# Reordering the input projections of a two-layer hybrid trunk, and storing the normalised gating values in DRAM

## The chip, the cores and the metric

The kernel runs on one core of a Trainium2 chip. The metric is the device time of one execution in microseconds; the median of a few runs stands for a kernel, and lower is better. One execution was also recorded by the hardware profiler, and all rows below come from that one.

## The reference

Two layers are applied to 1024 prompt tokens and 8 x 16 sample tokens (1152 columns), with D_MODEL 1024. Each layer is `x + w_out @ (concat(A, B, C, D) * silu(gates))`, and all inputs of the four branches and the gates come from one projection of `rms_norm(x)`.

- A is RWKV-7 time mixing. A token shift mixes each column with the one before; a decay `exp(-exp(w_log))` and a rate `a` come from two low-rank projections; the normalised keys kk enter as `-kk` and `kk*a`; the recurrence is

```python
sa = einsum('bhij,bhj->bhi', s, -kk_t)
s = s * w_t[:, :, None, :] + sa[:, :, :, None] * (kk_t * a_t)[:, :, None, :] + v_t[:, :, :, None] * k_t[:, :, None, :]
y = einsum('bhij,bhj->bhi', s, r_t)
```

- B is latent attention with a block-causal mask. The change does not touch it.
- C is spatial gating. The values are layer-normalised over their 256 features (`vn`, of which the sample part is an output), mixed within chunks of 128 positions by a lower-triangular 128x128 matrix per head, and multiplied into u.
- D is pooling: trailing means over 2, 4, 8 or 16 tokens minus the token, a small linear map per group and a scale.

## The kernel before

Features lie on partitions and tokens on columns, in three groups g of 384 columns. A layer has 24 input projections of 128 features each. WDAD holds the decay's and the rate's low-rank inputs, K0 K1, R0 R1 and V0 V1 are keys, receptances and values of A, D0 D1 the inputs of D, GD0 GD1 its gates, VC0 VC1 the gating values of C, U0 U1 its u, GC0 GC1 its gates. `F_ORDER` is the order in which `project` runs them and in which their weights are loaded. Arithmetic is float32: weights and inputs are split in a high and a low part, and each product is three matmuls (high by high, low by high, high by low), so a projection is 3 groups x 8 x 3 = 72 matmuls of 128x384. The weights come by SP's DMA queue in quarters of 128 KB (tile wr, three buffers), ACT copies the high part (wh, L241), POOL subtracts for the low part (wl, L242).

All other work is written as generators in three lanes, "a", "v" and "n". `project` calls `tick()` at the ticks that `inproj` gives it, and a tick runs each lane one step further, so a lane's instructions stand between the matmuls of the projection that runs at that time. Each engine then works its instructions off in order.

- Lane "a" first holds `a_elem`, the keys' chain, six per layer (two halves i, three groups g). It makes from w, a and k the four factors of the recurrence's matrices: `ar` (with -kk times the decay before the token, and later r times the decay), and `kb`. cs is the running sum of the decays within a chunk of 64, ex is exp(-cs), ei exp(+cs).
- `systems(g)` makes for each chunk of 64 tokens the matrix product that has to be inverted (tile ns, two buffers), masks it on DVE (L514) and stores it to DRAM (nd) by ACT's queue.
- `solve` loads them again, all side by side on partitions, inverts them on DVE by forward substitution (62 operations for 32 columns, L538 and L540; a smaller one for the samples first), copies the result transposed (L550) and stores both to DRAM (dd, L552 and L553) on ACT's queue.
- `recurrence` runs the 18 chunks, the two of the samples first. `prepare` loads a chunk's inverse (tt<-dd, L571, on SP), makes the masked products gm (L580) and the transposes kbt and vu (L590, L595), `advance` carries the state. `groupnorm` runs on lane "n" after chunks 5, 11 and 15.
- `normalise(j)` of lane "v" (L846 to L857) transposes a tile of 128 tokens of the gating values into a psum buffer (pool st, two buffers), takes mean and variance on DVE (L850, L852), scales (L855), and lets POOL apply the layer norm's weight and bias (L856, L857). The nine results stay in three m tiles; the m pool has eight buffers.

Psum has three pools: pj (2 buffers, the projections), st (2), b (4). `pool_in` computes D's windows on POOL and DVE, `silu` the gates on ACT (L756 to L758) and DVE.

Of the kernel before, what the change touches and what calls it, by code (L numbers as in the profile page):

```python
# [10 lines left out]
F32 = mybir.dt.float32  # L11
# [9 lines left out]
NS, SL = 8, 16  # L21
# [10 lines left out]
(WDAD, K0, R0, V0, K1, R1, V1, D0, GD0, D1, GD1, VC0, VC1, U0, GC0, U1, GC1,  # L32
 GB0, GB1, Q0, Q1K, CK, GA0, GA1) = range(NF)

F_ORDER = (WDAD, K0, K1, R0, R1, V0, V1, D0, GD0, D1, GD1, VC0, VC1, U0, GC0, U1, GC1,
           Q0, Q1K, CK, GB0, GB1, GA0, GA1)


# [10 lines left out]
def tile_trunk(ctx: ExitStack, tc: tile.TileContext, *aps):  # L49
# [37 lines left out]
    def nm(p):  # L87
        cnt[0] += 1
        return f"{p}_{cnt[0]}"
# [17 lines left out]
    def m_tile(cols=T):  # L107
        return mp.tile([128, cols], F32, tag="m", name=nm("m"))
# [16 lines left out]
    def go(lane, gen):  # L125
        lanes.setdefault(lane, deque()).append(gen)

    def start(lane, gen):
        next(gen)
        go(lane, gen)  # L130
# [15 lines left out]
    def finish(*names):  # L146
        while any([step(n) for n in names]):
            pass
# [8 lines left out]
    def gcols(g):  # L157
        return slice(g * G, (g + 1) * G)
# [186 lines left out]
    for l in range(L):  # L345
# [11 lines left out]
        def vcol(i):  # L357
            return vc[:, i:i + 1]
# [46 lines left out]
        def shifted(f, dest, after=None):  # L405
            inproj(f, shift_sink(f, dest, after))
# [17 lines left out]
        def chv(t):  # L424
            return t.rearrange("p (c s) -> p c s", s=64)

        def a_elem(i, g, k):
# [32 lines left out]
            if n < G:  # L460
                Po.tensor_copy(out=PendS[:, i, :].rearrange("p (c s) -> p c s", c=2),
                               in_=ex[:, nch:].rearrange("p c (s t) -> p c s t", t=SL)[:, :, :, SL - 1])
            V.tensor_tensor(out=rw, in0=cs, in1=rw, op=ALU.subtract)
            ep = rw
            A.activation(out=ep, in_=rw, func=AF.Exp, scale=-DECAY_C)
            ei = cs
            A.activation(out=ei, in_=cs, func=AF.Exp, scale=DECAY_C)
            yield

            kk = q  # L470
            V.scalar_tensor_tensor(out=kk, in0=k, scalar=vcol(V_KK + i), in1=q, op0=ALU.mult, op1=ALU.mult)
            V.scalar_tensor_tensor(out=ar[:, :, 0, :], in0=chv(kk), scalar=-1.0, in1=chv(ep),
                                   op0=ALU.mult, op1=ALU.mult)

            recip1p(av)
            yield
# [2 lines left out]
            for hh in range(2):  # L479
                pr = slice(64 * hh, 64 * hh + 64)  # L480
                V.tensor_tensor(out=kb[pr, :, hh, :], in0=chv(kk)[pr], in1=chv(t)[pr], op=ALU.mult)  # L481
            V.tensor_scalar(out=av, in0=av, scalar1=vcol(V_KA + i), scalar2=nv[:, 11 + i:12 + i],
                            op0=ALU.mult, op1=ALU.add)
            V.tensor_tensor(out=av, in0=av, in1=ei, op=ALU.mult)
            for hh in range(2):
                pr = slice(64 * hh, 64 * hh + 64)
# [336 lines left out]
            inproj(fg, sink_gd)  # L823


        def gating():
            sg = m_tile(1024)
            sgb = sg[:, 0:512].rearrange("p (a i t) -> p a i t", a=2, i=2)
            SY.dma_start(out=sgb, in_=sgub[l])
            sgg = sg[:, 512:1024].rearrange("p (a t) -> p a t", a=2)  # L830
            SY.dma_start(out=sgg, in_=sgugb[l])
            vraw = []
            for fv in (VC0, VC1):
# [3 lines left out]
                    A.activation(out=vr[:, gcols(g)], in_=ps, func=AF.Copy)  # L837
                inproj(fv, sink_v)
                vraw.append(vr)
            vn = [m_tile(1024), m_tile(1024), m_tile(1024)]  # L840

            def vnt(j):
                return vn[j // 4][:, (j % 4) * 256:(j % 4 + 1) * 256]

            def normalise(j):
                ps = st()[:, 0:256]  # L846
                for i in range(2):
                    PE.transpose(ps[:, i * 128:(i + 1) * 128], vraw[i][:, j * 128:(j + 1) * 128], ident)
                bs = smp.tile([128, 6], F32, tag="bs", name=nm("bs"))
                V.bn_stats(out=bs, in_=ps)  # L850
                mv = smp.tile([128, 2], F32, tag="mv", name=nm("mv"))
                V.bn_aggr(out=mv, in_=bs)  # L852
                rs = smp.tile([128, 1], F32, tag="rs1", name=nm("rs1"))
                rsqrt(rs, mv[:, 1:2], 1.0, ELN)
                V.tensor_scalar(out=vnt(j), in0=ps, scalar1=mv[:, 0:1], scalar2=rs, op0=ALU.subtract, op1=ALU.mult)  # L855
                Po.tensor_tensor(out=vnt(j), in0=vnt(j), in1=sgg[:, 0], op=ALU.mult)  # L856
                Po.tensor_tensor(out=vnt(j), in0=vnt(j), in1=sgg[:, 1], op=ALU.add)  # L857

            def norms():
                for j in range(9):  # L860
                    normalise(j)
                    if j % 2:
                        yield
                A.dma_start(out=vn_o[l], in_=vnt(8))
            go("v", norms())
            wst = m_tile(1024).rearrange("p (a h t) -> p a h t", a=2, h=4)
            SY.dma_start(out=wst[:, 0], in_=wsT[l])
            SY.dma_start(out=wst[:, 1], in_=wsS[l])
# [5 lines left out]
            for i, (fu, fg) in enumerate(((U0, GC0), (U1, GC1))):  # L874
# [2 lines left out]
                def sink_u(g, ps, u=u):  # L877
                    A.activation(out=u[:, gcols(g)], in_=ps, func=AF.Copy)
                inproj(fu, sink_u)
                finish("v")  # L880

                def sink_gc(g, ps, i=i, u=u):
                    t = silu(ps)
# [21 lines left out]
        def after_k1(g, zs):  # L905
            start("a", a_elem(1, g, zs))
            if g > 0:
# [2 lines left out]
        project([(l, WDAD), (l, K0)], xh, xl,  # L910
                [shift_sink(WDAD, lambda g: z6[:, gcols(g)], tanh_part),
                 shift_sink(K0, lambda g: zk0[:, gcols(g)], lambda g, zs: start("a", a_elem(0, g, zs)))])
        shifted(K1, lambda g: zk1[:, gcols(g)], after_k1)
        go("a", idle(4))
        go("a", systems(2))
        go("a", idle(4))
        go("a", solve())
        receptance(0, R0)
        receptance(1, R1)
        values(V0)  # L920
        values(V1)
        A.dma_start(out=shift_o[l], in_=sho)
        pool_in(0, D0)
        go("a", recurrence())
        pool_gate(0, GD0)
        pool_in(1, D1)
        pool_gate(1, GD1)
# [675 lines left out]
```

## Time and profile before

| | us |
|---|---|
| median of 3 runs | 1447.89 (1444.7 to 1640.55) |
| the profiled execution | 1447.32 |
| its span, first to last instruction | 1445.5 |
| PE busy | 1358.6 (94%) |
| DVE, ACT, POOL busy | 786.8, 746.6, 465.2 |
| mean granted clock of TensorE | 0.986 |

PE is the matrix engine (TensorE), DVE the vector engine, ACT the scalar engine, POOL GpSimd; SP and ACT issue DMAs. In rows, L12 is a line of the kernel, `a<-b` a tile written from a tile read, and a releaser is what ended an engine's idle time. A stretch of 72 matmuls is one projection; where it stands is read from the first matmul with its weights. In layer 0 WDAD and K0 (worked together) take 15.40 to 68.50, K1 to 90.70, R0 and R1 to 131.30, V0 and V1 to 159.30, D0 to 173.30, GD0 to 210.30; U0 takes 314.30 to 348.00. In layer 1 GD0 takes 885.30 to 922.10 and U0 1022.40 to 1055.20.

### The profile page before, as it was taken

How to read it: one execution, taken by the hardware profiler on the slowest of the kernel's cores; microseconds unless marked ns; L12 is line 12 of the kernel's file. 1: busy time of each engine (PE TensorE's matmuls, PEld its weight loads, DVE VectorE, ACT ScalarE, POOL GpSimd, SP SyncE). 2: the span in 40 equal slices, each digit the busy share in tenths (PEclk: the TensorE clock that was granted, in tenths of full speed). 3: DMA queues.
4: the chain of work that ended last, by engine and by line, in shares of the span. 5: the costliest groups of instructions: out<-in, count | busy, mean ns of one | idle time of the engine just before them, and what ended most of it. 6: DMA issues, size and time to landing. Idle time of an engine off the chain costs nothing. (4 is left out here: it accounts for less than half of the span.)

```text
span 1445.5 us, 26910 instructions
## 1 busy us (share of the span) xinstructions
PE 1358.6 (94%) x9962; PEld 1160.2 (80%) x9962; DVE 786.8 (54%) x1766; ACT 746.6 (52%) x2013; POOL 465.2 (32%) x600
## 2 busy tenths in 40 slices
PE   4899989999999999999989998999999999899999
PEld 3768868888988886679977788788789788766998
DVE  6984954435235567742287948444532374777211
ACT  6762234655466677642257621555654676866210
POOL 4514404336411033332162234232653111322320
PEclk9799999999999999999999999999999999999999
DMA  7113241110312214033300122321022111131232
GB/s 222 52 32 75 63 102 42 61 49 25 96 46 70 60 37 128 5 116 93 99 22 30 49 64 66 92 69 49 29 71 74 52 57 59 45 103 45 74 95 77
DMA packets 116596, 97.40 MB, mean 67 GB/s; under 512 B 46129, under 2 KB 111345, under 8 KB 116465
## 3 DMA queue, kind: packets, MB, share of 16 engines
q1 hardware_dynamic: 76776, 73.74, 17.6%
q10 hardware_dynamic: 39688, 21.94, 5.1%
q8 instruction: 79, 1.29, 0.4%
q14 instruction: 53, 0.43, 0.1%
HBM read 71.48 MB, written 24.16 MB: 66 GB/s over the span
## 5 line engine op out<-in xcount | busy, mean ns | idle before, releaser
L76 PE MATMUL pj<-xh,wh 128*128 128x384 f32 x1152 | 415.4, 361 | 18.9 <-ACT xh L280 7.2
L76 PE MATMUL pj<-xl,wh 128*128 128x384 f32 x1152 | 396.4, 344 | 2.4 <-POOL xl L282 2.0
L76 PE MATMUL pj<-xh,wl 128*128 128x384 f32 x1152 | 396.3, 344 | 0.0
L242 POOL TENSOR_TENSOR wl<-wr,wh 128x256 fp32r<-128x256 f32 x200 | 157.0, 793 | 465.9 <-ACT wh L241 390.5
L76 PEld LDWEIGHTS pj<-xh,wh 128*128 128x128 f32 x1152 | 221.6, 193 | 41.7 <-ACT sho L400 11.3
L76 PEld LDWEIGHTS pj<-xl,wh 128*128 128x128 f32 x1152 | 222.1, 193 | 9.0 <-POOL xl L282 3.3
L76 PEld LDWEIGHTS pj<-xh,wl 128*128 128x128 f32 x1152 | 221.4, 192 | 6.0 <-issue 4.8
L76 PE MATMUL pj<-yh,wh 128*128 128x384 f32 x384 | 129.3, 337 | 2.4 <-DVE x L1426 2.4
L76 PE MATMUL pj<-yh,wl 128*128 128x384 f32 x384 | 128.6, 335 | 0.0
L76 PE MATMUL pj<-yl,wh 128*128 128x384 f32 x384 | 128.3, 334 | 0.0
L241 ACT ACTIVATE wh<-wr 128x256 fp32r<-128x256 f32 x200 | 81.0, 414 | 84.7 <-PE pj L76 41.0
L242 POOL TENSOR_TENSOR wl<-m,wh 128x256 fp32r<-128x256 f32 x56 | 43.7, 790 | 102.0 <-ACT wh L241 84.4
L76 PEld LDWEIGHTS pj<-yh,wh 128*128 128x128 f32 x384 | 72.1, 188 | 3.7 <-DVE x L1426 2.8
L76 PEld LDWEIGHTS pj<-yl,wh 128*128 128x128 f32 x384 | 72.1, 188 | 0.1
L76 PEld LDWEIGHTS pj<-yh,wl 128*128 128x128 f32 x384 | 72.1, 188 | 0.1
L1293 ACT ACTIVATE X<-b,ng 128x512 f32<-128x512 f32 (+3 forms) x96 | 55.0, 577 | 25.3 <-DVE ng L1285 21.4
L76 PE MATMUL b<-sp,cr 128*128 128x384 f32 (+3 forms) x192 | 59.5, 385 | 3.2 <-POOL sp L99 2.8
L1281 DVE TENSOR_REDUCE mx<-b 128x1 f32<-128x512 f32 (+3 forms) x96 | 53.0, 556 | 9.8 <-PE b L76 8.0
L1422 DVE TENSOR_TENSOR pt<-pj,pt 128x384 f32<-128x384 f32 x24 | 13.4, 557 | 80.6 <-PE pj L76 80.6
L76 PEld LDWEIGHTS st<-X,X 128*64 128x64 f32 x576 | 35.1, 136 | 27.4 <-ACT X L1311 7.6
L241 ACT ACTIVATE wh<-m 128x256 fp32r<-128x256 f32 x56 | 22.4, 413 | 61.0 <-PE pj L76 59.9
L1304 PE MATMUL pj<-cm,X 128*128 128x128 f32 x288 | 48.0, 286 | 5.0 <-ACT X L1293 5.0
(307 smaller groups left out, 2591.7 us busy)
## 6 DMA issues: line engine op xcount, KB each, us to landing
wr<-in_win_dram SPq DMA_DIRECT2D x176, 128.0 KB
m<-in_wout_dram SPq DMA_DIRECT2D x12, 512.0 KB
x<-in_xT_dram SPq DMA_DIRECT2D x12, 384.0 KB
ysp<-m ACTq DMA_DIRECT2D x24, 192.0 KB
pt<-in_xT_dram SPq DMA_DIRECT2D x24, 192.0 KB
ea<-ysp SPq DMA_DIRECT2D x24, 192.0 KB
x1d<-x ACTq DMA_DIRECT2D x24, 192.0 KB
pt<-x1d SPq DMA_DIRECT2D x24, 192.0 KB
```

Of the source, the lines that this page charges most:

```text
L76: return PE.matmul(out, lhsT=lhsT, rhs=rhs, start=start, stop=stop, skip_group_check=True)
L241: A.activation(out=h, in_=r, func=AF.Copy)
L242: Po.tensor_tensor(out=lo, in0=r, in1=h.bitcast(F32), op=ALU.subtract)
L1281: V.tensor_reduce(out=mx[:, b:b + 1], in_=pc[:, :w], axis=AX.X, op=ALU.max)
L1293: A.activation(out=P[:, :w], in_=pc[:, :w], func=AF.Exp, scale=SCALE, bias=ng, accum_out=sums[pr][:, b, s, h:h + 1])
L1304: PE.transpose(ptp[:, j * 128:(j + 1) * 128], Pb[slot][:, j * 128:(j + 1) * 128], ident)
L1422: V.tensor_tensor(out=xr, in0=ps, in1=xr, op=ALU.add)
```

## The change

`F_ORDER` and the calls are put in a new order: V0 and V1 behind K0 and K1, VC0 and VC1 ahead of D0, and `recurrence` is launched behind the gating values, where it stood behind D0. In `a_elem` the decay before the token is no longer computed by its own subtraction and Exp: `ar` takes ex shifted by one column, and the first column of each chunk (and of each sample) is set to -kk by small DVE operations; one multiply-add moves from DVE to ACT. `gating` is cut in two. `gating_values` projects VC0 and VC1 and puts the normalising on lane "v"; a normalised tile stands in one of the three "gn" buffers and is stored to DRAM (vnd) by SP. `gating` finishes lane "v" and loads the nine tiles again.

```diff
@@ -32,7 +32,7 @@
 (WDAD, K0, R0, V0, K1, R1, V1, D0, GD0, D1, GD1, VC0, VC1, U0, GC0, U1, GC1,
  GB0, GB1, Q0, Q1K, CK, GA0, GA1) = range(NF)
 
-F_ORDER = (WDAD, K0, K1, R0, R1, V0, V1, D0, GD0, D1, GD1, VC0, VC1, U0, GC0, U1, GC1,
+F_ORDER = (WDAD, K0, V0, K1, V1, R0, R1, VC0, VC1, D0, GD0, D1, GD1, U0, GC0, U1, GC1,
            Q0, Q1K, CK, GB0, GB1, GA0, GA1)
 
 
@@ -460,17 +460,20 @@
             if n < G:
                 Po.tensor_copy(out=PendS[:, i, :].rearrange("p (c s) -> p c s", c=2),
                                in_=ex[:, nch:].rearrange("p c (s t) -> p c s t", t=SL)[:, :, :, SL - 1])
-            V.tensor_tensor(out=rw, in0=cs, in1=rw, op=ALU.subtract)
-            ep = rw
-            A.activation(out=ep, in_=rw, func=AF.Exp, scale=-DECAY_C)
             ei = cs
             A.activation(out=ei, in_=cs, func=AF.Exp, scale=DECAY_C)
             yield
 
             kk = q
             V.scalar_tensor_tensor(out=kk, in0=k, scalar=vcol(V_KK + i), in1=q, op0=ALU.mult, op1=ALU.mult)
-            V.scalar_tensor_tensor(out=ar[:, :, 0, :], in0=chv(kk), scalar=-1.0, in1=chv(ep),
+
+            V.scalar_tensor_tensor(out=ar[:, :, 0, 1:], in0=chv(kk)[:, :, 1:], scalar=-1.0, in1=ex[:, :, 0:63],
                                    op0=ALU.mult, op1=ALU.mult)
+            V.tensor_scalar(out=ar[:, 0:nch, 0, 0], in0=chv(kk)[:, 0:nch, 0], scalar1=-1.0, scalar2=None, op0=ALU.mult)
+            if n < G:
+                V.tensor_scalar(out=ar[:, nch:, 0, :].rearrange("p c (s t) -> p c s t", t=SL)[:, :, :, 0],
+                                in0=chv(kk)[:, nch:].rearrange("p c (s t) -> p c s t", t=SL)[:, :, :, 0],
+                                scalar1=-1.0, scalar2=None, op0=ALU.mult)
 
             recip1p(av)
             yield
@@ -479,8 +482,7 @@
             for hh in range(2):
                 pr = slice(64 * hh, 64 * hh + 64)
                 V.tensor_tensor(out=kb[pr, :, hh, :], in0=chv(kk)[pr], in1=chv(t)[pr], op=ALU.mult)
-            V.tensor_scalar(out=av, in0=av, scalar1=vcol(V_KA + i), scalar2=nv[:, 11 + i:12 + i],
-                            op0=ALU.mult, op1=ALU.add)
+            A.activation(out=av, in_=av, func=AF.Identity, scale=vcol(V_KA + i), bias=nv[:, 11 + i:12 + i])
             V.tensor_tensor(out=av, in0=av, in1=ei, op=ALU.mult)
             for hh in range(2):
                 pr = slice(64 * hh, 64 * hh + 64)
@@ -823,11 +825,11 @@
             inproj(fg, sink_gd)
 
 
-        def gating():
-            sg = m_tile(1024)
-            sgb = sg[:, 0:512].rearrange("p (a i t) -> p a i t", a=2, i=2)
-            SY.dma_start(out=sgb, in_=sgub[l])
-            sgg = sg[:, 512:1024].rearrange("p (a t) -> p a t", a=2)
+        vnd = dr.tile([9, 128, 256], F32, tag=f"vnd{l}", name=nm("vnd"))
+
+        def gating_values():
+
+            sgg = m_tile(512).rearrange("p (a t) -> p a t", a=2)
             SY.dma_start(out=sgg, in_=sgugb[l])
             vraw = []
             for fv in (VC0, VC1):
@@ -837,10 +839,6 @@
                     A.activation(out=vr[:, gcols(g)], in_=ps, func=AF.Copy)
                 inproj(fv, sink_v)
                 vraw.append(vr)
-            vn = [m_tile(1024), m_tile(1024), m_tile(1024)]
-
-            def vnt(j):
-                return vn[j // 4][:, (j % 4) * 256:(j % 4 + 1) * 256]
 
             def normalise(j):
                 ps = st()[:, 0:256]
@@ -852,17 +850,35 @@
                 V.bn_aggr(out=mv, in_=bs)
                 rs = smp.tile([128, 1], F32, tag="rs1", name=nm("rs1"))
                 rsqrt(rs, mv[:, 1:2], 1.0, ELN)
-                V.tensor_scalar(out=vnt(j), in0=ps, scalar1=mv[:, 0:1], scalar2=rs, op0=ALU.subtract, op1=ALU.mult)
-                Po.tensor_tensor(out=vnt(j), in0=vnt(j), in1=sgg[:, 0], op=ALU.mult)
-                Po.tensor_tensor(out=vnt(j), in0=vnt(j), in1=sgg[:, 1], op=ALU.add)
+                t = s_tile("gn", 3, 256)
+                V.tensor_scalar(out=t, in0=ps, scalar1=mv[:, 0:1], scalar2=rs, op0=ALU.subtract, op1=ALU.mult)
+                Po.tensor_tensor(out=t, in0=t, in1=sgg[:, 0], op=ALU.mult)
+                Po.tensor_tensor(out=t, in0=t, in1=sgg[:, 1], op=ALU.add)
+                SY.dma_start(out=vnd[j], in_=t)
+                if j == 8:
+                    SY.dma_start(out=vn_o[l], in_=t)
 
             def norms():
                 for j in range(9):
                     normalise(j)
                     if j % 2:
                         yield
-                A.dma_start(out=vn_o[l], in_=vnt(8))
             go("v", norms())
+
+        def gating():
+            finish("v")
+            sgb = m_tile(512).rearrange("p (a i t) -> p a i t", a=2, i=2)
+            SY.dma_start(out=sgb, in_=sgub[l])
+            vn = []
+            for a in range(3):
+                n = min(4, 9 - 4 * a)
+                vn.append(m_tile(1024))
+                SY.dma_start(out=vn[a][:, 0:256 * n].rearrange("p (j t) -> p j t", j=n),
+                             in_=vnd[4 * a:4 * a + n].rearrange("j p t -> p j t"))
+
+            def vnt(j):
+                return vn[j // 4][:, (j % 4) * 256:(j % 4 + 1) * 256]
+
             wst = m_tile(1024).rearrange("p (a h t) -> p a h t", a=2, h=4)
             SY.dma_start(out=wst[:, 0], in_=wsT[l])
             SY.dma_start(out=wst[:, 1], in_=wsS[l])
@@ -877,7 +893,6 @@
                 def sink_u(g, ps, u=u):
                     A.activation(out=u[:, gcols(g)], in_=ps, func=AF.Copy)
                 inproj(fu, sink_u)
-                finish("v")
 
                 def sink_gc(g, ps, i=i, u=u):
                     t = silu(ps)
@@ -910,18 +925,20 @@
         project([(l, WDAD), (l, K0)], xh, xl,
                 [shift_sink(WDAD, lambda g: z6[:, gcols(g)], tanh_part),
                  shift_sink(K0, lambda g: zk0[:, gcols(g)], lambda g, zs: start("a", a_elem(0, g, zs)))])
+        values(V0)
         shifted(K1, lambda g: zk1[:, gcols(g)], after_k1)
         go("a", idle(4))
         go("a", systems(2))
         go("a", idle(4))
         go("a", solve())
+        values(V1)
         receptance(0, R0)
         receptance(1, R1)
-        values(V0)
-        values(V1)
         A.dma_start(out=shift_o[l], in_=sho)
+        gating_values()
+        go("a", idle(4))
+        go("a", recurrence())
         pool_in(0, D0)
-        go("a", recurrence())
         pool_gate(0, GD0)
         pool_in(1, D1)
         pool_gate(1, GD1)
```

ACT at the end of the inversion in layer 0, before. m_1394 and m_1393 are the inverse and its transposed copy, pj psum of GD0, b that of the recurrence:

```order
L590 ACTIVATE kbt_1884<-b_1879 128x256
L595 ACTIVATE vu_1886<-b_1879 64x2x64 x2
L552 DMA dd_291<-m_1394 64x32x32
L553 DMA dd_291<-m_1393 64x32x32
L552 DMA dd_291<-m_1394 64x32x32
L553 DMA dd_291<-m_1393 64x32x32
L610 ACTIVATE m_1931<-b_1898 128x2x128 x2
L756 ACTIVATE pt_1940<-pj_1856 128x384
L636 ACTIVATE u_380_1954<-b_1949 128x128
```

and in the changed kernel; m_1501 and m_1500 are inverse and copy, m_1818 the values of VC1, wr and wh weights:

```order
L839 ACTIVATE m_1818<-pj_1845 128x384
L241 ACTIVATE wh_1880<-wr_1878 128x256
L241 ACTIVATE wh_1892<-wr_1890 128x256
L241 ACTIVATE wh_1904<-wr_1902 128x256
L554 DMA dd_291<-m_1501 64x32x32
L555 DMA dd_291<-m_1500 64x32x32
L554 DMA dd_291<-m_1501 64x32x32
L555 DMA dd_291<-m_1500 64x32x32
L241 ACTIVATE wh_1916<-wr_1914 128x256
L839 ACTIVATE m_1818<-pj_1871 128x384
L213 ACTIVATE rs_379_1943<-mv_1941,eps 128x1
```

The four stores of dd stood ahead of the recurrence's and GD0's work; now they stand between weight splits, ahead of the last group's copy of VC1 and of the normalising.

PE in the changed kernel, at the start of D0's second group (st_1975 and st_1990 are psum of normalise, m_1660 and m_1818 the values):

```order
L76 MATMUL pj_2054<-xh_333,wh_1758 128x384
L76 MATMUL pj_2054<-xl_334,wh_1758 128x384
L76 MATMUL pj_2054<-xh_333,wl_1759 128x384
L846 MATMUL st_1975<-cm,m_1660 128x128
L846 MATMUL st_1975<-cm,m_1818 128x128
L846 MATMUL st_1990<-cm,m_1660 128x128
L846 MATMUL st_1990<-cm,m_1818 128x128
L76 MATMUL pj_2054<-xh_333,wh_1758 128x384
```

The transposes of two tiles stand within the projection's first matmuls; before, they stood in U0.

DVE behind the inversion, before (u_380 and gm belong to the recurrence, pt to GD0's silu):

```order
L550 COPY m_1393<-m_1394 128x1024
L655 TENSOR_TENSOR u_380_1954<-b_1956,u_380_1954 128x128
L580 TENSOR_TENSOR gm_1964<-b_1965,cm 128x256
L759 TENSOR_TENSOR pt_1940<-pj_1856,pt_1940 128x384
L580 TENSOR_TENSOR gm_1964<-b_1969,cm 128x256
L820 SCALAR_TENSOR_TENSOR m_1717<-st_1945,vcs,pt_1940 128x384
```

and in the changed kernel (gn is the normalised tile, m_1922 the pooling of D0):

```order
L552 COPY m_1500<-m_1501 128x1024
L848 BN_STATS bs_1939<-st_1936 128x6
L848 BN_STATS bs_1954<-st_1951 128x6
L850 BN_AGGR mv_1941<-bs_1939 128x2
L850 BN_AGGR mv_1956<-bs_1954 128x2
L582 TENSOR_TENSOR gm_2107<-b_2108,cm 128x256
L582 TENSOR_TENSOR gm_2107<-b_2112,cm 128x256
L854 TENSOR_SCALAR gn_1946<-st_1936,mv_1941,rs_379_1943 128x256
L854 TENSOR_SCALAR gn_1961<-st_1951,mv_1956,rs_384_1958 128x256
L793 SCALAR_TENSOR_TENSOR m_1922<-pt_2012,pinv_t,m_1921 64x384
L848 BN_STATS bs_1978<-st_1975 128x6
```

The statistics of the first two tiles now come first behind the inversion's copy, and the recurrence's first products between them and the scaling.

## Rows read from the trace of the kernel before

**Rows 1.** The page's first part: busy time, share of the span, instructions of each engine.

```profile
PE 1358.6 (94%) x9962; PEld 1160.2 (80%) x9962; DVE 786.8 (54%) x1766; ACT 746.6 (52%) x2013; POOL 465.2 (32%) x600
```

**Rows 2.** Stretches: start:end length, busy PE PEld DVE ACT POOL, clock, DMA share, GB/s.

```profile
15.40:68.50 53.10, 43.34 (x165) 35.13 (x165) 49.32 (x78) 39.07 (x94) 25.56 (x23) 0.88 0.34 90
68.50:90.70 22.20, 21.43 (x97) 16.59 (x96) 16.45 (x30) 14.27 (x38) 6.12 (x10) 0.90 0.08 25
90.70:131.30 40.60, 37.30 (x284) 30.79 (x285) 28.86 (x62) 18.32 (x45) 11.88 (x16) 1.00 0.18 54
131.30:159.30 28.00, 25.89 (x147) 24.93 (x146) 18.87 (x67) 7.65 (x23) 10.09 (x17) 1.00 0.33 75
159.30:173.30 14.00, 12.70 (x73) 12.38 (x72) 13.49 (x32) 3.37 (x9) 6.74 (x11) 1.00 0.27 73
173.30:210.30 37.00, 30.32 (x313) 25.77 (x311) 25.16 (x56) 12.62 (x41) 8.96 (x13) 0.95 0.40 79
...
151.90:186.80 34.90, 29.70 (x224) 27.64 (x223) 33.17 (x83) 7.22 (x21) 14.57 (x20) 0.98 0.25 56
314.30:348.00 33.70, 31.05 (x350) 25.97 (x349) 19.84 (x52) 20.00 (x73) 22.23 (x28) 0.95 0.08 25
650.00:700.00 50.00, 50.00 (x291) 50.00 (x290) 13.39 (x24) 12.55 (x28) 11.87 (x16) 1.00 0.35 97
885.30:922.10 36.80, 31.26 (x312) 26.60 (x310) 25.04 (x56) 12.62 (x41) 8.77 (x13) 0.91 0.38 80
1022.40:1055.20 32.80, 29.75 (x351) 24.86 (x350) 20.44 (x53) 20.07 (x73) 22.26 (x28) 1.00 0.09 26
```

**Rows 3.** PE's waits, in 60:115, 160:235, 314:348: us in all, times, longest.

```profile
PE b L76 <- DVE m L397: 2.6, 1, 2.6
...
PE b L76 <- DVE gm L580: 3.2, 2, 3.0
...
PE st L848 <- DVE m L855: 1.8, 1, 1.8
```

**Rows 4.** Instruction groups of DVE, 20:115: busy us, mean ns | idle before.

```profile
L463 DVE TENSOR_TENSOR ea<-ea,ea 128x384 f32<-128x384 f32 x6 | 3.9, 652 | 0.1
L482 DVE TENSOR_SCALAR ea<-ea,vcs,nv 128x384 f32<-128x384 f32 x6 | 3.9, 649 | 0.1
...
L397 DVE SCALAR_TENSOR_TENSOR m<-sh,vcs,m 128x8 f32<-128x8 f32 x3 | 0.7, 221 | 0.0
```

**Rows 5.** The chain that ended last, in 815:840: start, us, what.

```profile
833.20 3.06 DMA nd<-ns
```

**Rows 6.** Timeline of DVE, 131:190: start, us, instruction, idle before and releaser.

```profile
143.11 0.16 DVE L538 TENSOR_TENSOR m<-m 32x15 f32<-32x15 f32 x1 [0.86 <-POOL wl L242]
...
186.85 1.07 DVE L550 COPY m<-m 128x1024 f32<-128x1024 f32 x1
```

**Rows 7.** Timeline of ACT, 183:201.

```profile
193.14 0.66 ACT L610 ACTIVATE m<-b 128x256 f32<-128x256 f32 x2 [14.66 <-issue]
```

**Rows 8.** Timeline of SP, 183:201.

```profile
197.03 0.50 SPq L571 DMA_DIRECT2D tt<-dd  x1
```

**Rows 9.** Instruction groups of DVE, 151.9:186.85.

```profile
L538 DVE TENSOR_TENSOR m<-m,m 128x31 f32<-128x31 f32 (+15 forms) x31 | 13.5, 435 | 0.8
L540 DVE TENSOR_TENSOR m<-m,m 128x31 f32<-128x31 f32 (+15 forms) x31 | 13.2, 424 | 0.8
```

**Rows 10.** The same with shapes kept apart.

```profile
L538 DVE TENSOR_TENSOR m<-m,m 128x220 f32<-128x220 f32 x2 | 1.6, 810 | 0.1
...
L538 DVE TENSOR_TENSOR m<-m,m 128x252 f32<-128x252 f32 x2 | 0.8, 411 | 0.0
```

**Rows 11.** Instruction groups of all engines in U0, 314:348.

```profile
L857 POOL TENSOR_TENSOR m<-m,m 128x256 f32<-128x256 f32 x9 | 6.9, 771 | 0.6
L856 POOL TENSOR_TENSOR m<-m,m 128x256 f32<-128x256 f32 x9 | 6.8, 756 | 2.8 <-DVE m L855 2.0 <-DVE mv L852 0.7
...
L855 DVE TENSOR_SCALAR m<-st,mv,rs 128x256 f32<-128x256 f32 x9 | 4.6, 532 | 0.4 <-ACT rs L214 0.4
```

## The prediction

> **What bounds the kernel now.** I read the busy times first. PE works 1358.6 of 1445.5 us [rows 1], so only about 87 us are idle, and nothing in this change takes matmuls away. It can win PE's waits, and the time in which PE ran at the lower clock, and it can make new ones. So the second view was PE by stretch, one stretch per projection [rows 2]. The reader should compare three columns: length, PE busy (their difference is idle time) and the granted clock. In an undisturbed stretch 291 matmuls take 50.00 us, 0.172 each, so that one input projection of 72 costs 12.4 us; the rest of a stretch is recurrence work, waits, or lower clock. Four places lie over that:
>
> - WDAD and K0: 53.1 us for 165 matmuls, DVE busy 49.3 of it. K1 behind it has clock 0.90.
> - V0, V1 and D0 together 3.4 us idle, under the inversion.
> - GD0: 6.7 us idle and clock 0.95 in layer 0, 5.5 us and 0.91 in layer 1. Idle plus what the clock lost (0.05 x 37.0, 0.09 x 36.8) gives 8.5 and 8.8 us.
> - U0: 2.65 and 3.05 us idle.
>
> The third view, PE's waits by what ended them, names the causes [rows 3]: a wait of 2.6 us for DVE behind the keys' chain, 3.2 us for the recurrence's products (gm, in GD0), and 1.8 us in U0 for the normalised tile that frees a psum buffer. The GD0 row misleads until one looks at the instructions: gm's line is late because DVE was in the inversion, and because ACT stood behind it.
>
> **Keys' chain.** Each of the six chains of a layer loses one DVE subtract (0.652 us) and one ACT Exp, and moves a DVE multiply-add (0.649) to ACT [rows 4]. It gains one or two DVE operations on six or fewer columns; the nearest row is 128x8 at 0.221. The large multiply stays. Per chain DVE gets about 0.652 + 0.649 - 1.5 x 0.22 = 1.0 us back and ACT nothing (one out, one in). Six chains make 6 us per layer, but only where PE waits for DVE does that count. In layer 0 that is the 2.6 us wait, and the half clock behind it, worth 0.10 x 22.2 = 2.2 us in K1. V0's projection now stands between K0 and K1, so that the third chain of K0 has 12 us more cover. Lower bound 0 (DVE is equally full with x's normalisation), upper -5 (wait and clock both gone); I take -2 in layer 0. In layer 1 PE's wait there is not ended by this chain; bounds 0 and -0.6, I take -0.3.
>
> **Values between the keys.** V0 and V1 have no chains, and they move forward past K1, R0 and R1; their work is the same. The K1-dependent systems(0) and systems(1) get more ticks before R0. R0 and R1 (90.70 to 131.30) have 3.3 us idle; a part of it is the ring of the systems: 18 products ns, each stored by ACT's queue, with two buffers, so each waits for the store two before, of 3.06 us [rows 5]. That ring is unchanged. Bounds +2 (the shift operations of V0 and V1 fall into the DVE-heavy stretch) and -3 (all the idle time goes); I take -1 per layer.
>
> **Inversion, and what covers it.** Before, it starts at 143.11, and the copy behind its last step at 186.85 [rows 6]: 43.7 us. GD0 starts at 173.30, so DVE is 13.5 us late, and ACT then issues four dd stores and is free only at 193.14 [rows 7], 6.3 us behind the copy's start; the first reader of dd is issued at 197.03 [rows 8]. After, the recurrence starts only behind VC1. Before that, systems(2) is done by about the end of R1's first column group, thanks to V1's extra ticks, and I put the inversion's start 5 us behind that. Its length: in the big part's 34.9 us (151.90 to 186.80) DVE is busy 33.17 [rows 2], of which the 62 outer products and adds are 13.5 + 13.2 = 26.7 [rows 9]; the other 6.5 are other work (shifts of V1, pooling of D0). Nor do the 62 run evenly: two of 128x220 took 0.810 each, two of the larger 128x252 only 0.411 [rows 10]. Taking for each of the 31 shapes its shortest time in either layer, they would sum to 20.7, an estimate; so some 6 us come from operations stretched beyond that, where POOL is busy 14.57 us. VC0 and VC1 bring DVE nothing and POOL only weight splits. So the inversion takes between some 30 us (43.7 - 6.5 - 6, and a little more from the small part) and 43.7; I take 34, half of the stretching staying, since the splits stay. End: 39 us behind R1's first group. PE by then has done 2/3 of R1 (10) and two bare projections (24.8), 34.8: the inversion ends about 5 us behind VC1.
>
> What is queued behind it: ACT's order has the four dd stores ahead of one weight split and VC1's last copy out of psum. That copy frees the psum buffer that D0's second group needs. It is over at 6.3 + 0.41 + 0.5 = 7.2 us behind the inversion, so 12 us behind VC1, and PE has D0's first group (4.1) and the first transposes, some 6 us in all, for that: 6 us idle. Then the normalise tiles stand close together, interleaved with the first products of the recurrence and pooling, on PE's two st buffers: another 4. With 1.4 left elsewhere and 1 of clock that is 12.4 us per layer, where before there are 8.5 + 3.4 = 12: **+0.5** per layer. With a lag of 1 it is -5, with the old length of 43.7 it is +10; both ends are kept.
>
> **Normalising out of U0.** Nine tiles per layer, 18 POOL operations at 0.76 (13.7 us) and nine DVE ones at 0.53 [rows 11], leave U0 and go into D0. PE's idle time in U0 (2.65, 3.05) goes for the most part: -2.5, bounds 0 and -4 (idle and clock). The POOL time lands beside D0's windows; its cost is in the term above.
>
> **Recurrence later, reload.** It starts one projection later and still ends within U1 and GC1. Three reloads of up to 512 KB and nine stores of 128 KB go through SP, where the weights' loads queue; GC0 needs the first reload. In U0 DMA has a share of 0.08 [rows 2], so there is room; but SP's load of S0 now waits behind dd. +0.5 per layer, bounds 0 and +4.
>
> **Sum.** Layer 0: -2 - 1 + 0.5 - 2.5 + 0.5 = -4.5. Layer 1: -0.3 - 1 + 0.5 - 2.5 + 0.5 = -2.8. Together -7.3 on the profiled 1447.3 (median of the runs 1447.9): **1440**. Its own range is 1430 to 1450. About 2% (29 us) is what a measurement here tells from no change, so faster is under 1418 and slower over 1476.
>
> **Rivals.** *Inversion hidden entirely* (chance 0.18). It takes 30 us and ends with VC1; D0 then flows. That saves 6.5 more per layer: 1440 - 13 = **1427**, and 1415 with every term at its best end. For it: DVE and POOL have little else in VC0 and VC1. Against: the dd stores still block ACT.
>
> *The normalise chain runs dry on its buffers* (0.15; the slower side). A tile now holds one of three gn buffers until its store has landed, where before it was left in place. One round costs DVE 0.53 + POOL 1.53 + landing 3.06 (the store of ns, half its size) = 5.1 us, and nine tiles need two further rounds: 10.2 us per layer, if transposes come closer than 1.7 us apart and nothing else keeps PE busy. 1440 + 20.4 = **1460**. It decides once D0's transposes are bunched, which PE's order shows them to be behind a late inversion; to be slower by 2% it needs 18 us per layer. Against: PE can run D0's matmuls between, if the psum buffers allow it.
>
> The Trainium skill ("SBUF — State Buffer", The DMA setup-cost knee) says that every transfer pays a roughly fixed 2 us and that a loop of small transfers per tile runs far under the rate of one large one; it speaks against a DRAM round trip tile by tile. With its figures a 128 KB store is an estimated 2.3 us, and this rival would come to 8.7 us per layer, 1457. The trace's own store of 3.06 us is the one used above.
>
> *Late reload or psum and m-tile pressure in GC0 to U1* (0.07): the m pool has eight buffers and U1 would like nine, so U1's tile waits for GC0's last reader: about 4 us per layer in place of 0.5, **1447**, up to 1455.
>
> *The chain change does nothing, and the rest also cancels*: within the forecast's range, no own case.
>
> Chances: forecast 0.60, hidden 0.18, buffers 0.15, pressure 0.07. Range **1416 to 1461**: it reaches the first rival's low end and the second's middle. Faster by over 2%: half of the hidden case's lower part and a little of the forecast's tail, 0.13. Slower by over 2%: a third of the buffers case, and a little for bounds that all go wrong, 0.07. The rest, 0.80, is within 2%.
>
> **What would show it.** PE's table by projection: GD0 without its idle time and at clock 1.00, U0 idle under 1, D0 long (about 24 us for the forecast, under 18 for the first rival, over 33 for the second). The inversion's first and last step against the end of VC1. PE's waits in D0: by ACT's copy out of VC1 (the dd stores) or by DVE's normalised tile (L854 of the changed kernel, the gn ring). I am wrong if D0 shows no wait, or if the time moved outside WDAD to GC1 of either layer.

## The result, and the profile after

The changed kernel takes 1454.95 us (median of 15 runs, 1451.83 to 1459.65) against 1447.1 of the kernel before (15 runs; one of them, 1640.55, stands far apart and does not enter the ratio). The ratio is **1.0057, interval 1.0044 to 1.0070**: slower by 0.6%. I had said 1440, faster by 0.5%. The time lies within my range, but the direction was wrong.

The profiled execution took 1457.11, its span is 1455.3: 9.8 us longer than before. The first part of its page, and the clock's row (each digit is a fortieth of the span, 9 full speed):

```profile
PE 1358.6 (93%) x9962; PEld 1159.5 (80%) x9962; DVE 788.2 (54%) x1758; ACT 747.2 (51%) x2013; POOL 465.2 (32%) x600
...
PEclk9899989999999999999989998999999999999999
```

PE is busy for the same 1358.6 us as in [rows 1]. That is two effects in balance: less time per matmul in one place, more matmuls at half clock in another. So I read the stretches, now cut at the changed order's projections. First the columns of [rows 2] for V0 to R1 of both layers before (K1 to V1 there) ...

```profile
68.50:159.30 90.80, 84.62 (x526) 72.32 (x526) 64.18 (x158) 40.24 (x105) 28.09 (x40) 0.97 0.20 54
782.00:871.30 89.30, 82.50 (x527) 70.70 (x527) 64.85 (x160) 41.83 (x109) 28.25 (x40) 1.00 0.21 55
```

... and the changed kernel: WDAD and K0; V0 to R1; VC0 and VC1; D0; GD0; U0 of layer 0; then one stretch within D0; then V0 to R1, VC0, D0, GD0 and U0 of layer 1.

```profile
14.90:68.00 53.10, 40.39 (x163) 31.55 (x163) 47.75 (x76) 38.89 (x93) 26.43 (x23) 0.95 0.36 95
68.00:151.30 83.30, 81.63 (x527) 72.05 (x527) 50.13 (x115) 41.31 (x107) 26.09 (x36) 0.97 0.22 58
151.30:177.90 26.60, 25.28 (x146) 24.96 (x146) 24.59 (x72) 6.41 (x16) 7.77 (x11) 1.00 0.18 49
177.90:212.50 34.60, 22.93 (x203) 19.54 (x202) 23.64 (x58) 9.52 (x36) 19.61 (x30) 0.85 0.40 90
212.50:244.80 32.30, 29.13 (x324) 23.62 (x322) 16.01 (x33) 14.36 (x47) 8.63 (x13) 0.95 0.33 81
300.70:331.10 30.40, 29.27 (x383) 24.51 (x381) 12.26 (x29) 17.12 (x61) 6.46 (x8) 1.00 0.17 52
...
185.40:195.80 10.40, 3.62 (x12) 3.10 (x13) 5.07 (x13) 2.54 (x10) 3.30 (x4) 0.51 0.72 113
781.60:863.40 81.80, 79.68 (x527) 70.00 (x527) 48.97 (x114) 41.46 (x108) 25.65 (x36) 1.00 0.23 59
863.40:880.50 17.10, 14.34 (x74) 14.02 (x73) 15.63 (x49) 3.79 (x10) 6.27 (x8) 0.90 0.19 51
893.00:926.00 33.00, 23.01 (x205) 19.61 (x204) 22.56 (x55) 9.52 (x36) 19.61 (x30) 0.90 0.40 95
926.00:957.80 31.80, 29.22 (x323) 23.94 (x321) 15.48 (x32) 14.37 (x47) 8.61 (x13) 0.95 0.31 82
1013.20:1047.50 34.30, 30.20 (x382) 25.34 (x380) 11.06 (x29) 15.26 (x57) 5.24 (x6) 0.95 0.15 46
```

The reader should see a gain and a loss. V0 to R1 gives back 7.5 us in each layer (90.8 to 83.3, 89.3 to 81.8). D0 now holds 203 matmuls (73 in [rows 2]; the rest are the recurrence's and the transposes) and 11.7 us of idle time at clock 0.85; GD0, which held 6.7 us idle in [rows 2], still has 3.2 at 0.95; and U0 of layer 1 has 4.1. PE's waits in WDAD and K0, in VC0 to D0, in GD0 to GD1, and in layer 1's U0 say by what:

```profile
PE b L76 <- DVE m L397: 4.3, 1, 4.3
...
PE pj L76 <- ACT m L839: 8.3, 1, 8.3
PE st L846 <- DVE gn L854: 3.3, 3, 1.4
...
PE b L76 <- DVE m L668: 3.2, 1, 3.2
...
PE b L76 <- DVE u L657: 4.1, 1, 4.1
```

L397 is a token shift of the sample columns, L839 VC1's copy out of psum, L854 the scaled normalised tile, L668 and L657 are steps of the recurrence. The timelines show the wait for L839, in order POOL, ACT (queue, then engine), PE:

```profile
185.11 0.11 POOL L775 MEMSET m<- 128x15 f32 x1 [6.66 <-DVE m L542]
...
185.09 0.66 ACTq L554 DMA_DIRECT2D dd<-m  x1
186.16 0.89 ACTq L555 DMA_DIRECT2D dd<-m  x1
187.07 2.55 ACTq L554 DMA_DIRECT2D dd<-m  x1
189.66 1.55 ACTq L555 DMA_DIRECT2D dd<-m  x1
...
191.33 0.42 ACT L241 ACTIVATE wh<-wr 128x256 fp32r<-128x256 f32 x1 [13.70 <-issue]
191.66 0.47 ACT L839 ACTIVATE m<-pj 128x384 f32<-128x384 f32 x1
...
192.18 0.69 PE L76 MATMUL pj<-xh,wh 128*128 128x384 f32 x1 [8.29 <-ACT m L839]
```

ACT stands at the dd stores from 177.6 until the inversion ends (185.1), issues them until 191.2 (the second waits for the transposed copy), and only then empties the psum buffer that D0's second group needs. This is the wait forecast. The POOL row holds one that was not: D0's own input tile (m) comes free only with the inversion's end.

### The profile page after: what moved, and what is told of

Its sections match the earlier page's. It is cut to its first block, busy times and chain, and to the rows that moved or that the text cites. A ratio compares the mean times of both kernels' runs of the same rounds, so it can differ in the third digit from the quotient of the medians.

```text
span 1455.3 us, 26970 instructions
## 1 busy us (share of the span) xinstructions
PE 1358.6 (93%) x9962; PEld 1159.5 (80%) x9962; DVE 788.2 (54%) x1758; ACT 747.2 (51%) x2013; POOL 465.2 (32%) x600
## 4 chain that ended last, share of the span: by engine, by line
PE 70%; DVE 15%; ACT 4%; DMA 4%; POOL 3%; issue 3%; ACTq 1%; SPq 0%; DVEq 0%; POOLq 0%
PE pj L76 41%; PE b L76 16%; PE st L76 9%; PE pj L1321 3%; DVE m L540 2%; DVE ea L278 2%; DVE m L542 2%; DMA nd<-ns 2%; POOL pt L786 1%; DVE ea L170 1%; PE b L588 1%; POOL gn L855 1%; DVE gn L730 1%; DMA nds<-ns 1%; DVE xl L282 1%
```

## The experiments

Ratios are to the kernel before, with 95% intervals; e6 and e7 are single runs and have none. The diffs show the lines that matter, not the whole edits.

**e1, the old keys' chain in the new order.**

```diff
+V.tensor_tensor(out=rw, in0=cs, in1=rw, op=ALU.subtract)
+A.activation(out=ep, in_=rw, func=AF.Exp, scale=-DECAY_C)
-A.activation(out=av, in_=av, func=AF.Identity, scale=vcol(V_KA + i), bias=nv[:, 11 + i:12 + i])
+V.tensor_scalar(out=av, in0=av, scalar1=vcol(V_KA + i), scalar2=nv[:, 11 + i:12 + i],
+                op0=ALU.mult, op1=ALU.add)
```

> The changed kernel with the keys' chain as before (subtract, second Exp and the multiply-add on DVE back), order of projections kept. Theory A (the 7.5 us that K0 to R1 gained in each layer come from the order: V0 and V1 give DVE time between the keys): at most 2 us slower than the changed kernel, 1455 to 1457, with V0 to R1 still 82 to 85 us per layer. Theory B (they come from the shorter chain): V0 to R1 back to 89 us per layer, 1467 to 1471.

1459.49, 1.0079 (1.0055 to 1.0103). V0 to R1 takes 87.0 us in layer 0 and 85.7 in layer 1: between the theories, with the time nearer to theory A. The interval overlaps the changed kernel's, so the chain's share is read from the stretch and not from the time.

**e2, the new chain alone in the old order.** The chain's lines of the change in the kernel before.

> The kernel before with only the shorter keys' chain. Theory A: 1444 to 1447 (before 1447), K1 to V1 of layer 0 at 88 to 91 us, the gain at most the half clock in K1. Theory B: 7 us less in each layer, 1432 to 1435.

1443.77, 0.9976 (0.9957 to 0.9996). K1 to V1 takes 91.0 and 88.2 us (90.8 and 89.3 before); the gain of 4 us is just clear of the noise, and spread out.

**e3, only V0 and V1 between the keys**, all else as before.

```diff
-F_ORDER = (WDAD, K0, K1, R0, R1, V0, V1, D0, GD0, D1, GD1, VC0, VC1, U0, GC0, U1, GC1,
+F_ORDER = (WDAD, K0, V0, K1, V1, R0, R1, D0, GD0, D1, GD1, VC0, VC1, U0, GC0, U1, GC1,
```

> The kernel before with only V0 and V1 moved between the keys; the old chain, gating values behind GD1 as before. The inversion then has only R1's end and D0 in front of GD0. Theory A: V0 to R1 take 82 to 85 us in place of 90; the inversion ends about 20 us behind D0 instead of 13.5, so GD0 loses some 6 us more per layer: 1444 to 1448. Theory B: no gain in V0 to R1, GD0 loses 6 more: 1459 or above.

1465.39, 1.0121 (1.0084 to 1.0159). The profiled execution took 1471.80. The first stretch is V0 to R1, then GD0 and D1 of layer 0:

```profile
66.90:152.60 85.70, 83.39 (x526) 73.26 (x526) 54.39 (x119) 41.48 (x109) 25.73 (x38) 0.96 0.21 55
166.70:195.00 28.30, 23.05 (x193) 20.30 (x191) 27.08 (x61) 8.37 (x23) 9.62 (x13) 0.88 0.20 44
195.00:241.00 46.00, 41.53 (x414) 34.30 (x413) 19.22 (x42) 15.37 (x59) 13.26 (x20) 0.78 0.34 81
```

From e1 and e3 the order gives 3.2 to 5.1 us per layer in V0 to R1, and the chain on top of it (83.3 against 87.0, 81.8 against 85.7) 3.7 to 3.9. Neither theory was right alone. The missing cover costs more than I expected: GD0 and D1 of layer 0 have 9.7 us idle and lose 13 to 14 more to the clock (0.88 and 0.78). So this order needs other work to cover the inversion; in the change VC0 and VC1 are that work.

**e4, the dd stores behind VC1's last copy on ACT.**

```diff
+behind(copies[-1], stores)   # copies[-1] is VC1's last copy, stores the four dd stores
```

> The changed kernel with the four dd stores put behind VC1's last copy on ACT. Theory C (ACT's order makes D0's loss): the wait of D0's second group for that copy (8.3 and 6.6 us) goes; the third group then waits some 4 us for D0's first copy, which still stands behind the stores. D0's idle time falls from 11.7 and 10.0 to 6 to 8, total 1446 to 1449. Theory D (the normalise chain and DVE behind the inversion set D0's length): the wait moves to the normalise tiles, less than 2 us per layer gained, 1451 to 1455.

1458.14, 1.0071 (1.0045 to 1.0098): no gain, and outside both forecasts. D0, and a stretch in it, and PE's two waits there (L814 is D0's copy out of psum, L860 the statistics of a tile):

```profile
176.30:208.50 32.20, 24.81 (x174) 22.08 (x173) 19.07 (x50) 6.70 (x25) 17.57 (x26) 0.73 0.40 92
...
190.00:207.20 17.20, 13.29 (x101) 11.27 (x101) 9.31 (x20) 4.93 (x19) 14.04 (x21) 0.50 0.36 97
```

```profile
PE pj L76 <- ACT m L814: 4.2, 1, 4.2
PE st L856 <- DVE mv L860: 3.2, 1, 3.2
```

The wait fell as theory C said (idle in D0 from 11.7 to 7.4), but then PE worked at 1.2 GHz from 190.0 to 207.2, where the changed kernel did so from 185.4 to 195.8 with most of that stretch idle. What the wait gave, the clock took.

**e5, the normalising held back to D1 and GD1.**

```diff
+go("v", idle(18))
 go("v", norms())
```

> The changed kernel with the normalising lane held back by 18 ticks, so that its nine tiles stand in D1 and GD1 in place of D0; everything else as in the changed kernel. Theory C (D0's loss is the late inversion and ACT's order): the 8 us wait for VC1's last copy stays, D0 and GD0 together lose 1 to 3 us less per layer, total 1450 to 1456. Theory D (the bunched normalise tiles set D0's length, 3.3 us of waits for gn and half clock behind them): D0 and GD0 lose 6 to 9 us less per layer (idle and clock of 21.6 and 17.7 down to 13), total 1438 to 1445.

1471.80, 1.0174 (1.0153 to 1.0196). D1 of layer 0:

```profile
222.30:276.50 54.20, 47.52 (x565) 38.05 (x563) 30.17 (x73) 22.86 (x95) 26.36 (x37) 0.84 0.30 93
```

Theory D's local part held: D0 and GD0 lose 6.9 and 6.5 us less than in the changed kernel, in idle time and clock together (counted as in the table further down). But D1, which lost 0.1 us, now loses 14.6 and 16.2. The loss moved and grew: beside the running recurrence the nine tiles cost more than in D0.

**e6, two more buffers for normalised tiles.**

```diff
-t = s_tile("gn", 3, 256)
+t = sm[:, 256 * (j - 1):256 * j] if j in (3, 4) else s_tile("gn", 3, 256)
```

> The changed kernel with two more buffers for normalised tiles (tiles 3 and 4 stand in unused columns of the tile that holds the layer norm's weight), so that the ring of three is waited for later. Theory C: PE's waits for gn in D0 fall from 3.3 to under 2, the sum of idle and lost clock in D0 and GD0 hardly moves, 1453 to 1457. Theory D's ring variant (my rival of the prediction): the gn waits go and the stretch shortens by 4 to 6 us per layer, 1443 to 1447.

One run, 1453.77. D0 of layer 0, and its waits:

```profile
178.50:215.80 37.30, 24.55 (x205) 21.08 (x204) 25.17 (x62) 9.73 (x36) 22.03 (x32) 0.82 0.40 93
```

```profile
PE b L588 <- ACT u L638: 3.4, 1, 3.4
...
PE st L847 <- DVE gn L855: 1.0, 1, 1.0
```

The gn waits went (3.3 to 1.0) and a wait of 3.4 us for the recurrence took their place; D0 is no shorter. So far as one execution shows, the ring of three, my slower rival, is not what cost the time; e12 below shows no clear gain from the two buffers either. Its price by the Trainium skill ("SBUF — State Buffer", The DMA setup-cost knee) came to 1457, near the measured time, but the trace does not bear out that mechanism: with fewer waits for gn D0 stays as long.

**e7 and e9, the recurrence launched behind D0**, one run and then timed.

```diff
-go("a", idle(4))
-go("a", recurrence())
 pool_in(0, D0)
+go("a", recurrence())
```

> The changed kernel with the recurrence launched behind D0, one projection later. Theory C: D0's wait for VC1's copy stays (8 us), the recurrence's own waits in GD0 (3.2 and 2.6 us for the samples' DVE work) shrink as dd has long landed, its end moves into GC1: 1452 to 1458. Theory E (the recurrence's first products in D0 and GD0 are the loss, being fed by a DVE that is full of normalising): 1443 to 1449.

> The same kernel as the one look at the recurrence behind D0 (1441.7), now timed. Theory F (the recurrence launched ahead of D0 is what costs the change its gain: its first steps meet a DVE, an ACT and a POOL that are behind the inversion and the normalising, and every later step follows late, at half clock): the median is 1440 to 1444, ratio to the kernel before 0.994 to 0.998, against 1.0057 of the changed kernel. If that look was a lucky clock, 1446 to 1452.

e7 1441.68; e9 1442.11, 0.9963 (0.9950 to 0.9976). D0 and GD0 of layer 0 in e9, and the first part of its page (of an execution of 1445.41):

```profile
178.70:210.90 32.20, 20.47 (x103) 17.63 (x102) 21.36 (x54) 7.03 (x29) 17.54 (x27) 0.80 0.40 90
210.90:238.30 27.40, 26.96 (x300) 22.77 (x299) 14.44 (x31) 11.92 (x37) 10.47 (x16) 0.98 0.37 97
...
PE 1356.7 (94%) x9962; PEld 1160.9 (80%) x9962; DVE 779.9 (54%) x1758; ACT 747.6 (52%) x2013; POOL 464.5 (32%) x600
```

D0 still has its waits (8.5 us for VC1's copy, 3.2 for gn). What went are the waits behind it: GD0 0.4 us idle in place of 3.2, U0 of layer 1 none in place of 4.1. This one move turns the change from 0.6% slower to 0.4% faster, about 13 us. It removed two things at once: DVE's wait of 4.4 us for a mask's load in layer 1 is gone too, and e13 below prices that load by itself at 4.7 us. So an estimated 8 of the 13 us (13 less 4.7) are the launch's own.

**e8, four moves at once**: recurrence behind D0, dd stores behind D0's second copy, normalising in GD0, mask load ahead of GD1.

> The changed kernel with four moves: dd stores behind D0's second copy on ACT, recurrence launched behind D0, the normalising begun in GD0, and the triangle mask of the gating weights loaded ahead of GD1. VC0, VC1 and D0 then all cover the inversion. Theory C: no wait in D0 at all, D0 about 13 us, D0 and GD0 with under 8 us of idle and lost clock, U0 without the 4.1 us wait of layer 1; the gain is 10 to 12 us per layer less what the recurrence's later end costs in GC1 and Q0 (0 to 8): 1432 to 1445, below the kernel before. If the losses only move (to GD0, D1 or the tail, by waits and half clock), 1448 to 1456.

1445.73, 0.9993 (0.9980 to 1.0006). D0 and GD0:

```profile
177.60:190.10 12.50, 12.50 (x74) 12.50 (x74) 7.66 (x21) 2.21 (x5) 5.43 (x9) 1.00 0.31 65
190.10:229.10 39.00, 31.36 (x277) 25.40 (x277) 25.88 (x59) 14.31 (x53) 22.31 (x33) 0.87 0.42 103
```

D0 flows without any wait, as expected, and GD0 takes the loss (5.4 us for gn, clock 0.87). The time falls just outside the first forecast's range and short of the second's. e11 below, which begins the normalising in D0's second group and leaves the mask alone, takes 1434.06; so it is the normalising beside the recurrence's start that undoes the gain here.

**e10 and e11, the recurrence behind D0, normalising begun with D0's second group**, and the dd stores on SP (e10) or on ACT behind D0's second copy (e11).

```diff
+go("v", idle(3))
-A.dma_start(out=diagonal(dd, i, 32, 128), in_=DT[64 * i:64 * i + 64])
+SY.dma_start(out=diagonal(dd, i, 32, 128), in_=DT[64 * i:64 * i + 64])   # e10, and DN's store alike
+behind(copies[-1], stores)   # e11: copies[-1] is D0's second copy
```

> The recurrence behind D0, and two moves more: the four dd stores issued by SP in place of ACT, the normalising begun with D0's second group. Theory C' (with the recurrence out of the way, ACT's 8 us behind the inversion are the largest loss left in D0): the wait for VC1's copy goes, D0 falls from 32 and 29 us to 20 to 24, total 1425 to 1434. Theory D' (DVE reaches the normalising only after the inversion, whatever ACT does): the wait moves to the normalise tiles in st, total 1436 to 1444.

> As the one with dd stored by SP, but the stores stay on ACT, behind D0's second copy out of psum. Theory C': the stores are interleaved with the normalising's small ACT operations, so those wait up to 6 us: D0 loses 3 to 5 us, GD0 2 to 4, total 1430 to 1438. Theory D': 1436 to 1444.

e10 1438.68, 0.9930 (0.9904 to 0.9956); e11 1434.06, 0.9900 (0.9881 to 0.9920). Here, with the recurrence out of the way, taking ACT's block out of D0 and beginning the normalising a third of D0 later do pay: 8 us less than e9 in e11. No run parts the two moves. e10 came out as theory D' said, with gn waits of 4.6 and 9.0 us in the two layers; its five runs lie far apart (1431.92 to 1444.85), and these waits are from the one of 1444.85.

**e12, e11 with the two more buffers.**

> The version with the recurrence behind D0, the dd stores behind D0's second copy on ACT and the normalising begun with D0's second group, and in addition two more buffers for normalised tiles. Theory G (the 5 to 6 us per layer that PE still waits for normalised tiles come from the ring of three): those waits fall under 2 us, total 1426 to 1431. Theory H (they come from DVE and ACT behind the inversion): waits stay, 1432 to 1437.

1431.69, 0.9894 (0.9877 to 0.9910), not clearly apart from e11. D0 and GD0 of layer 0:

```profile
178.50:195.90 17.40, 15.34 (x83) 14.89 (x82) 12.85 (x36) 3.96 (x15) 10.03 (x15) 0.90 0.25 57
195.90:233.10 37.20, 30.30 (x319) 25.13 (x319) 20.77 (x47) 14.97 (x50) 18.37 (x28) 0.95 0.58 122
```

This version beats both kernels, by 1.1% and 1.6%. Waits of 6.0 and 4.4 us for normalised tiles stay, as theory H said. The longest, 3.9 us in each layer, is for no gn buffer. PE waits there for the scaling (L865) that frees its psum tile, and on DVE that stands directly behind four pooling operations of D0 (L803), with no idle time between:

```profile
202.76 2.59 DVE L803 SCALAR_TENSOR_TENSOR m<-pt,pinv_t,m 64x384 f32<-64x384 f32 x4
205.38 0.99 DVE L865 TENSOR_SCALAR gn<-st,mv,rs 128x256 f32<-128x256 f32 x2
...
206.07 0.41 PE L857 MATMUL st<-cm,m 128*128 128x128 f32 x2 [3.92 <-DVE gn L865]
```

**e13, only the mask's load ahead of GD1** in the changed kernel.

```diff
 pool_in(1, D1)
+tri_ = [s_tile("pt", 4, 256)]
+SY.dma_start(out=tri_[0], in_=cstt)
 pool_gate(1, GD1)
```

> The changed kernel with only the load of the triangle mask of the gating weights put ahead of GD1. Theory I (in layer 1's U0 DVE waits 4.4 us for this load, and the recurrence's step behind it on DVE makes PE wait 4.1): U0 of layer 1 falls from 34.4 to 29 to 31 us, total 1449 to 1452. Theory J (the recurrence is late anyway): the wait goes to the next step, 1453 to 1456.

1450.22, 1.0021 (1.0007 to 1.0034), 4.7 us under the changed kernel; layer 1's U0 falls from 34.3 to 28.5. DVE's timeline of the changed kernel shows why:

```profile
1018.85 0.69 DVE L888 TENSOR_TENSOR m<-m,pt 128x512 f32<-128x512 f32 x1 [4.37 <-DMA pt<-in_cstt_dram]
...
1020.59 0.28 DVE L657 TENSOR_TENSOR u<-b,u 128x128 f32<-128x128 f32 x1
```

The mask's tile is one of the four buffers of GD1's silu; U0 now follows GD1 directly, so the load comes late, DVE waits 4.4 us, and the recurrence's step stands behind it. Before, VC0 and VC1 lay between. Here taking one wait away did give its time.

**e14 and e15, one of the two POOL operations per normalised tile on DVE**, in the changed kernel and in e12.

```diff
-Po.tensor_tensor(out=t, in0=t, in1=sgg[:, 0], op=ALU.mult)
+V.tensor_tensor(out=t, in0=t, in1=sgg[:, 0], op=ALU.mult)
```

> The changed kernel with the layer norm's multiplication of the nine tiles on DVE in place of POOL; nothing else. Theory K (behind the inversion POOL is the serial resource of D0: 13.7 us of normalising and 6.7 us of pooling windows in one queue, 19.6 of 34.6 us busy, and the chain that ended last goes through it from 193 to 205): POOL has 7 us less to do, DVE 5 to 6 more; D0 and GD0 fall by 3 to 6 us per layer, total 1444 to 1450. Theory L (ring, ACT or the recurrence alone set D0's length): 1453 to 1457, or slower, as DVE gets more.

> The fastest version so far (1431.7) with that multiplication on DVE too. Theory K: there the chain goes through the load of S0 and PE, POOL hardly shows in it, so it gives 0 to 3 us: 1428 to 1432. Theory L: 1431 to 1436.

e14 1452.55, 1.0035 (1.0016 to 1.0055); e15 1432.71, 0.9903 (0.9870 to 0.9936), the same as e12. The reason for e14 was the chain that ended last in the changed kernel, which runs through POOL in D0:

```profile
193.10 0.85 POOL pt L786
193.96 0.69 POOL gn L855
...
203.18 0.72 POOL gn L856
203.90 0.82 POOL pt L786
```

Halving that work gave 2.4 us, less than theory K's least. gn's waits fell to 0.9 us, and the next wait was there: 1.2 us for the load of S0. The intervals of e14 and the changed kernel overlap. So POOL's work alone is not shown to set D0's length.

## Why the prediction was wrong

The terms per layer, in us, idle time plus lost clock where a stretch changed its content. Positive is slower. The lost clock is counted for PE's busy time only, since idle time at the lower clock is idle time already: the stretch of 10.4 us at clock 0.51 in D0 has 3.62 us of work, so it loses 1.8 us to the clock.

| step | forecast, layer 0 / 1 | measured |
|---|---|---|
| K0 to R1: chain and values between | -3 / -1.3 | -7.5 / -7.5 |
| inversion's cover: VC, D0, GD0 | +0.5 / +0.5 | +7.8 / +10.9 |
| U0 | -2.5 / -2.5 | -3.2 / +2.8 |
| D1, GD1, GC0 to GC1 | +0.5 / +0.5 | +2.0 / +3.4 |
| from WDAD to GC1, all | -4.5 / -2.8 | -0.2 / +8.8 |

The measured terms add up to the last row within 1 us. About 1 us more lies behind GC1, where layer 1's attention has a stretch at the lower clock that the kernel before did not have. Neither of my two signs of being wrong came: D0 shows the waits, and the time moved within WDAD to GC1. They tested where the time moves; what failed was mainly its price.

**Keys' chain, values between.** Right in sign, too small, and by other waits than the one I named. e1 and e3 show that both halves give about 4 us per layer in the new order, the chain too in layer 1, where I had it at 0.3. The wait that I counted, 2.6 us for L397, did not go (4.3 us now), and the half clock of K1 came back in V0 (2.2 us there, 0.13 x 18.2 = 2.4 now). What went are eight shorter waits behind it, for the systems' masks and the token shifts, which I had passed over: PE's idle time in the whole stretch fell from 6.2 to 1.7 us in layer 0 and from 6.8 to 2.1 in layer 1. The other 3 us are matmuls that ran closer together.

**Inversion and cover: the step that failed.** Its first half held. In layer 0 the inversion took 37.8 us (forecast 34); it ended 7.2 and 5.4 us behind VC1 (forecast 5, though 39 less 34.8 is 4.2), PE then waited 8.3 and 6.6 us for VC1's copy (forecast 6), and 3.3 and 3.4 for gn (forecast 4). Its rows, to be set beside [rows 9]; the time in the stretched operations fell, as forecast:

```profile
L540 DVE TENSOR_TENSOR m<-m,m 128x31 f32<-128x31 f32 (+15 forms) x31 | 12.4, 401 | 1.1
L542 DVE TENSOR_TENSOR m<-m,m 128x31 f32<-128x31 f32 (+15 forms) x31 | 11.9, 385 | 1.1
```

What failed is the rest of the sum, "1.4 left elsewhere and 1 of clock", for which I had named no row. In place of 12.4 us, VC0 to GD0 lose 19.5 and 20.5: the half clock costs 3.3 and 5.2 us (1 forecast), GD0 keeps 3.2 and 2.6 us of idle time, which I had set to nothing, and the wait for VC1's copy is 2.3 and 0.6 us longer than forecast.

**Recurrence later: the other half of the failure.** I costed its launch by where it ends (+0.5 per layer, GC1). What counted is what lies beside its first steps. Before, they stood in GD0, beside a gate's silu; now they stand in D0 with the pooling windows and the nine normalised tiles, while DVE, ACT and POOL are all behind. e9 moves this launch alone, and about 13 us come back for both layers; the estimated 8 of them that are not the mask's are the whole distance to the kernel before (7.85). That is 4 per layer where I had 0.5. The loss does not sit in one wait of D0. e4, e6 and e14 each shortened one, and the time moved by +3, -1 and -2.4 us, none clear of the noise; starting the consumer later (e9), and then making room on ACT with the normalising later (e11), brought it back. Which of the three engines holds up the recurrence's first steps the most, no run isolates.

**Normalising out of U0.** Right in layer 0 (-3.2). In layer 1 the mask's load took the place of the wait removed, which no term of mine had; e13 shows it.

**Rivals.** Hidden inversion: no, it ended 5 to 7 us late, and e8 shows that a free D0 alone is not enough. Buffers running dry: its time, 1460, was the nearest, but by luck: the gn waits were 3.3 and 3.4 us where it had 10.2, and two more buffers gained nothing clear of the noise (e6, e12). Pressure in GC0 to U1: its upper end, 1455, is the measured time, but there are no waits over 0.6 us there.

The mean granted clock is 0.979 in the profiled executions of e9 and of the changed kernel alike; their spans differ by 11.7 us, PE's idle time by 9.8 (96.7 against 86.9), so that the launch cost idle time, not clock. Moving the launch and the mask's load together, and nothing else, was not tried, and neither was keeping the normalised tiles in SBUF during D0.

## What to carry to other kernels

When work is moved to lie beside a late event, list for each in-order engine what stands behind that event and add it up. Waits in series can hide one another: in D0, taking one away gave nothing clear of the noise, and starting the consumer that meets all of them later did. A wait that stands alone, as that for the mask, gives its time. That load was late because its rotating buffer's last user had moved next to it; when an order changes, look for such loads and issue them ahead. And when idle time and lost clock are added, count the clock only for the time in which the engine works.

## What the runs showed of the hardware

A shorter wait need not be a shorter time. In the changed kernel PE was idle in most of a stretch of 10.4 us at clock 0.51; with that wait halved (e4) it worked through 17.2 us at 0.50, and the sum stayed. Issuing the four dd stores of 256 KB took 0.66, 0.89, 2.55 and 1.55 us of ACT's queue, and in the changed kernel no ACT instruction ran between them; on SP's queue (e10) they took 0.62, 0.60, 2.62 and 1.35.
